# Background steps of the recurrent stage emitted at the same priority as the matrix products

## The chip, the cores and the metric

The kernel runs on one core of a Trainium2 chip. The metric is the device time of one execution in microseconds (us), the median of three runs. The engines are named as the profile names them: PE (TensorE matmul), PEld (TensorE weight load, which overlaps PE), DVE (VectorE), ACT (ScalarE), POOL (GpSimd) and SP (SyncE, which here only issues DMAs).

## The reference, cut to what matters

The whole network has two layers of mixer, cross attention and convolutional feed-forward, and then one `hybrid_layer` on 256 positions of width 1024. The change lies in that last layer:

```python
def hybrid_layer(x, ...):
    xn = rmsnorm(x, norm_mix)
    (u_rnn, u_gate, q, k_c, v_c, k_s, v_s, k_w, v_w, g_nsa, g_a, g_b) = split(xn @ w_in)
    h_a = rg_lru(causal_depthwise_conv(u_rnn, conv_w, conv_b), gate_a_w, gate_a_b, gate_x_w, gate_x_b, lru_lambda)
    y_a = h_a * gelu(u_gate)                       # recurrent branch
    y_b = nsa_mixer(q, k_c, v_c, k_s, v_s, k_w, v_w, g_nsa, ...)   # sparse attention, 16 heads
    merged = sigmoid(g_a) * (y_a @ proj_a) + sigmoid(g_b) * (y_b @ proj_b)
    h = x + merged @ w_out
    z = rmsnorm(h, norm_mlp) @ w_mlp_in
    return h + square(relu(z)) @ w_mlp_out

def rg_lru(x, w_a, b_a, w_x, b_x, lam):            # 4 blocks of 336 channels
    r, i = sigmoid(block_diag(x, w_a, b_a)), sigmoid(block_diag(x, w_x, b_x))
    log_a = -8 * r * softplus(-lam)
    u = sqrt(-expm1(2 * log_a)) * (i * x)          # first position: factor 1
    h_t = exp(log_a_t) * h_{t-1} + u_t             # scan over 256 positions
```

In `nsa_mixer` the keys and values are also compressed: `compress_blocks` runs overlapping blocks of 32 positions through a small network (`gelu(flat @ w1) @ w2`), and `rmsnorm` scales the compressed keys. Each head's scores against compressed, selected and window keys go through one softmax each, and the three results are added under gates.

## The kernel before, in words

**Products.** Each matrix product is in fp32r, split into a high and a low half on both sides, so each k step takes three matmuls (L410 to L412, `fmh`/`fml` times `wh`/`wl`). The weights are streamed by the class `Stream`. SP loads a tile (`raw`, four buffers), ACT casts it to `wh` (L220), DVE subtracts to get `wl` (L221), with four buffers of each half. `w.take(key)` hands out the next tile, and keeps the cast and the subtraction two tiles ahead of the product.

**The recurrent stage.** `block2` runs `lru_steps` over four blocks of 336 channels. A block takes 3 `ur` products (the convolution follows: one ACT activation L1295 and three DVE operations L1298 for each), 3 `ug` products (the GELU: ACT L1313 and L1315, DVE L1314 and L1316), and then the two gates, `lga` and `lgx`, each three products of 9 matmuls that ACT empties by L1328. When a block's gates are there, `lru_tail` is put on the list of background steps: exponentials (L1340), DVE L1341, tanh (L1345), a square (L1347), DVE L1348, a square root (L1350, which brings an ACT_TABLE_LOAD), DVE L1351 and L1352, the scans (L1355), L1357, and the split into `yah` (ACT L396) and `yal` (DVE L397).

**The other background steps.** `phi_steps` compresses keys and values: 8 chunks of weights in the main loop, and then as a background step the GELU on ACT (L1222, with a table load), transposes to PE and two DVE copies of one shape (L1228, L1232), the small products (L1236 for the keys, L1244 for the values), a reciprocal root by three DVE operations (L384 to L386) and 12 POOL operations (L388 to L391), the DVE scaling L1254, the transpose L1258, and the split into `ks`, whose low half is DVE L397. `nsa_units`, driven by `attend`, gives the attention: `scores` of a head pair and 128 queries, then four ticks later `probs_t` (ACT copies L1435, L1445 `pct`), two ticks later `sums` (L1454, whose result is split into a low half and `fmh`, ACT L396). In `scores`, PE computes L695 and L696, DVE adds the bias and takes the maximum (L1398 to L1411), ACT takes six exponentials (L1417), DVE scales (L1419 to L1423).

**What follows.** `ga` products (emptied by ACT L1599 into `macc`), `pa`, `gb`, `pb`, the output product and the MLP.

**Order.** PE runs in the order of the program text. The order on ACT, DVE, POOL and SP is set by a scheduler at build time, which issues ready instructions by priority; inside `high_priority(offset=n)` an instruction ranks as if written n steps earlier. Each `take` calls `tick`. It runs the `later` steps that are due (`probs_t` and `sums` among them) at an offset of `DUE` = 10, and one step of each generator in `self.back` (the tail of `phi_steps`, `lru_tail`, `attend` with `scores`) at an offset of `BACK` = 20.

Of the kernel before, what the change touches and what calls it, by code (L numbers as in the profile page):

```python
# [42 lines left out]
BACK = 20  # L43
# [130 lines left out]
class Stream:  # L174
# [3 lines left out]
    def __init__(self, tc, pool, dram, order, tick, ahead=2, raw=4, parts=4):  # L178
        self.tc, self.nc, self.pool, self.dram, self.order = tc, tc.nc, pool, dram, order
        self.after, self.until, self.tick = (), 0, tick  # L180
        self.place = {}
        self.ahead, self.raw, self.parts = ahead, raw, parts
        self.whole = ("pkv",)
        self.n = self.loaded = self.split = 0
        self.raws, self.hl = {}, {}
# [70 lines left out]
class Program:  # L256
    def __init__(self, ctx, tc, a, out):
        self.ctx, self.tc, self.nc, self.a, self.out = ctx, tc, tc.nc, a, out
        nc = self.nc
        self.base = ctx.enter_context(tc.tile_pool(name="base", bufs=1))  # L260
        self.ps = ctx.enter_context(tc.tile_pool(name="ps", bufs=1, space=bass.MemoryType.PSUM))
        wpool = ctx.enter_context(tc.tile_pool(name="w", bufs=1))
        order = []

        def add(key, lo=0, hi=None):
            n = a[key].shape[0]
            order.extend((key, c) for c in range(lo, n if hi is None else hi))

        for l in range(L1):
            if l == 0:  # L270

                add("kv0", 0, 1)
                add("qa0", 0, 1)
            for key in ("kv", "qa", "v", "u", "qb"):
                add(f"{key}{l}", 1 if l == 0 and key in ("kv", "qa") else 0)
            for b in (2, 0, 1):
                for n in range(4 * b, 4 * b + 4):
                    add(f"gate{l}", 2 * n, 2 * n + 2)
                    add(f"br{l}", n, n + 1)
            add(f"mix{l}")  # L280
            add(f"wq{l}")
            add(f"wk{l}", 2 * l, 4)
            add(f"wv{l}")
            add(f"wo{l}")
            if l == 0:
                add("wk1", 0, 1)
            add(f"upb{l}")
            add(f"up{l}")
            if l == 0:
                add(f"down{l}")  # L290
                add("wk1", 1, 2)
            else:
                for c in range(NFF):
                    for q in range(len(EARLY)):
                        if EARLY[q] == c:
                            add("q2", q, q + 1)
                    add(f"down{l}", c, c + 1)
        self.order2(add)
        self.now, self.due, self.back, self.prev = 0, [], [], None
        self.w = Stream(tc, wpool, a, order, self.tick)  # L300
        self.ident = self.base.tile([128, 128], F32, name="ident")
        make_identity(nc, self.ident)

        warm = self.sc((128, 128))
        for _ in range(WARM):
            nc.tensor.matmul(warm, self.ident, self.ident, start=True, stop=True)
# [42 lines left out]
    def tick(self):  # L349

        self.now += 1
        due = [d for d in self.due if d[0] <= self.now]
        self.due = [d for d in self.due if d[0] > self.now]
        with self.tc.high_priority(offset=DUE):
            for _, fn in due:
                fn()
        for g in list(self.back):
            with self.tc.high_priority(offset=BACK):
                if next(g, self) is self:
                    self.back.remove(g)  # L360

# [1113 lines left out]
    def block2(self, x, xs, outs):  # L1475
        nc, tc, w, a = self.nc, self.tc, self.w, self.a
        with ExitStack() as st:
# [98 lines left out]
            yb = self.fm()  # L1576
            phi = self.phi_steps(zts, w2, [k[:, :, 256:271] for k in ks], vcz, kcg)
            self.phi_done = False
            self.tbp = st.enter_context(tc.tile_pool(name="tbp", bufs=1))
            self.back.append(self.attend(self.nsa_units(qt, ks, v, vcz, gt, pcs, yb), *NSA))  # L1580
            with tc.tile_pool(name="lru", bufs=1) as lp:
# [100 lines left out]
```

## Time and profile before

| | before |
|---|---|
| runs | 1436.12 us median (1435.93 to 1438.66) |
| profiled execution | 1439.39 us, span 1437.6 us |
| PE busy | 1415.7 us (98% of the span), 9919 matmuls |
| PEld busy | 1289.7 us (90%) |
| DVE busy | 1083.4 us (75%) |
| ACT busy | 891.7 us (62%) |
| POOL busy | 47.0 us (3%) |
| PE's clock | 9 tenths or more in each of 40 slices; 1.00 from 980 to 1200 us |

PE's share says that the time is a sum of matmuls and of the few waits between them. The other engines' shares are means over the span. The recurrent stage, where the change acts, runs from about 980 to 1115 us, and the profile is read there.

### The profile page before, as it was taken

What the parts mean: (1) busy time and instruction counts of PE and PEld (TensorE: products, weight loads), DVE (VectorE), ACT (ScalarE), POOL (GpSimd) and SP (SyncE); (2) the same over time, 40 slices, a digit from 0 to 9 for tenths busy, and PEclk for the clock granted to TensorE, in tenths of its full rate; (3) what the DMA queues carried; (4) which work ended last, traced back from release to release, by engine and by line L of the source; (5) the groups of instructions that cost most, each with busy time, mean ns of one, the idle gap of its engine ahead of it and who ended that gap; (6) DMA issues with size and microseconds to landing.
All of it is one profiled execution on the core that took longest, in us unless ns stands there. A gap on an engine that the chain in (4) does not pass through costs nothing.

```text
span 1437.6 us, 26028 instructions
## 1 busy us (share of the span) xinstructions
PE 1415.7 (98%) x9919; PEld 1289.7 (90%) x9919; DVE 1083.4 (75%) x2196; ACT 891.7 (62%) x1609; POOL 47.0 (3%) x143
## 2 busy tenths in 40 slices
PE   8999999999999999999999999999999999999998
PEld 6899988899988899998889998788989999899987
DVE  6997676788857898668679986786789785866543
ACT  5876556666645486655667665464898775555432
POOL 1110000000000020000000000120100000000000
PEclk9999999999999999999999999999999999999999
DMA  8454564555556544455636557356544445645563
GB/s 316 166 191 148 191 220 136 187 187 192 182 193 218 180 152 152 137 204 175 220 132 213 196 198 260 110 171 190 167 131 142 133 145 176 208 154 197 191 206 103
DMA packets 75335, 257.63 MB, mean 179 GB/s; under 512 B 9803, under 2 KB 11211, under 8 KB 75083
## 3 DMA queue, kind: packets, MB, share of 16 engines
q1 hardware_dynamic: 75211, 255.97, 54.3%
q8 instruction: 78, 1.28, 0.3%
q14 instruction: 46, 0.38, 0.1%
HBM read 254.89 MB, written 1.05 MB: 178 GB/s over the span
## 4 chain that ended last, share of the span: by engine, by line
PE 83%; DVE 6%; ACT 5%; DMA 3%; issue 1%; POOL 1%; SPq 0%; DVEq 0%; ACTq 0%; POOLq 0%
PE mm L410 16%; PE mm L411 15%; PE mm L412 15%; PE mm L426 8%; PE mm L424 8%; PE mm L425 8%; DVE wl L221 2%; PE mm L467 2%; PE mm L469 2%; PE mm L470 2%; ACT wh L220 1%; PE tp L772 1%; PE tp L733 1%; DMA raw<-in_kv_dram 1%; PE sc L695 1%
## 5 line engine op out<-in xcount | busy, mean ns | idle before, releaser
L220 ACT CAST wh<-raw 128x1024 fp32r<-128x1024 f32 (+3 forms) x432 | 446.5, 1038 | 373.0 <-PE mm L411 124.4
L221 DVE TENSOR_TENSOR wl<-raw,wh 128x1024 fp32r<-128x1024 f32 (+3 forms) x432 | 518.0, 1204 | 210.8 <-ACT wh L220 202.3
L410 PE MATMUL mm<-fmh,wh 128*128 128x256 f32 (+1 forms) x1736 | 487.0, 281 | 2.8 <-ACT macc L1599 1.5
L412 PE MATMUL mm<-fmh,wl 128*128 128x256 f32 (+1 forms) x1736 | 483.5, 278 | 0.0
L411 PE MATMUL mm<-fml,wh 128*128 128x256 f32 (+1 forms) x1736 | 483.4, 278 | 0.0
L410 PEld LDWEIGHTS mm<-fmh,wh 128*128 128x128 f32 (+1 forms) x1736 | 324.9, 187 | 8.1 <-issue 2.9
L412 PEld LDWEIGHTS mm<-fmh,wl 128*128 128x128 f32 (+1 forms) x1736 | 324.5, 187 | 0.0
L411 PEld LDWEIGHTS mm<-fml,wh 128*128 128x128 f32 (+1 forms) x1736 | 323.7, 186 | 0.2
L424 PE MATMUL mm<-wh,fmh 128*128 128x512 f32 x200 | 79.7, 398 | 2.0 <-ACT wh L220 1.3
L425 PE MATMUL mm<-wl,fmh 128*128 128x512 f32 x200 | 78.6, 393 | 0.8 <-DVE wl L221 0.8
L426 PE MATMUL mm<-wh,fml 128*128 128x512 f32 x200 | 78.8, 394 | 0.0
L425 PE MATMUL mm<-wl,ah 128*128 128x512 f32 x164 | 63.8, 389 | 0.0
L426 PE MATMUL mm<-wh,al 128*128 128x512 f32 x164 | 63.8, 389 | 0.0
L424 PE MATMUL mm<-wh,ah 128*128 128x512 f32 x164 | 63.8, 389 | 0.0
L410 PE MATMUL mm<-oh,wh 128*128 128x256 f32 x192 | 54.1, 282 | 0.0
L412 PE MATMUL mm<-oh,wl 128*128 128x256 f32 x192 | 53.5, 279 | 0.0
L411 PE MATMUL mm<-ol,wh 128*128 128x256 f32 x192 | 53.5, 279 | 0.0
L425 PE MATMUL mm<-wl,zh 128*128 128x512 f32 x128 | 49.8, 389 | 0.0
L424 PE MATMUL mm<-wh,zh 128*128 128x512 f32 x128 | 49.8, 389 | 0.0
L426 PE MATMUL mm<-wh,zl 128*128 128x512 f32 x128 | 49.8, 389 | 0.0
L1086 ACT ACTIVATE k<-mm,featp 128x256 f32<-128x256 f32 x88 | 48.5, 558 | 0.0
L424 PEld LDWEIGHTS mm<-wh,fmh 128*128 128x128 f32 x200 | 37.6, 188 | 10.1 <-ACT wh L220 1.8
(406 smaller groups left out, 2638.3 us busy)
## 6 DMA issues: line engine op xcount, KB each, us to landing
raw<-in_up_dram SPq DMA_DIRECT2D x80, 512.0 KB, 4.3
raw<-in_gate_dram SPq DMA_DIRECT2D x48, 512.0 KB, 3.5
raw<-in_down_dram SPq DMA_DIRECT2D x44, 512.0 KB, 4.3
raw<-in_mout_dram SPq DMA_DIRECT2D x32, 512.0 KB, 4.3
raw<-in_min_dram SPq DMA_DIRECT2D x28, 512.0 KB, 4.3
raw<-in_br_dram SPq DMA_DIRECT2D x24, 512.0 KB, 3.6
raw<-in_mix_dram SPq DMA_DIRECT2D x16, 512.0 KB, 3.7
raw<-in_wo_dram SPq DMA_DIRECT2D x16, 512.0 KB, 3.5
```

Of the source, the lines that this page charges most:

```text
L220: self.nc.scalar.copy(h[:p, :w], r[:p, :w])
L221: self.last = self.nc.vector.tensor_sub(l[:p, :w], r[:p, :w], h[:p, :w].bitcast(F32))
L410: self.nc.tensor.matmul(ps, wh[:kw, c], xh[k], start=start and k == 0, stop=False)
L411: self.nc.tensor.matmul(ps, wh[:kw, c], xl[k], start=False, stop=False)
L412: self.nc.tensor.matmul(ps, wl[:kw, c], xh[k], start=False, stop=stop and k == n - 1)
L424: self.nc.tensor.matmul(outs[t], xh[:, k, r], wh[:, c], start=k == 0, stop=False)
L425: self.nc.tensor.matmul(outs[t], xh[:, k, r], wl[:, c], start=False, stop=False)
L426: self.nc.tensor.matmul(outs[t], xl[:, k, r], wh[:, c], start=False, stop=k == k_all - 1)
L467: self.nc.tensor.matmul(outs[t], xl[:, k, r], wh, start=False, stop=k == 7)
L469: self.nc.tensor.matmul(outs[t], xh[:, k, r], wh, start=k == 0, stop=False)
L470: self.nc.tensor.matmul(outs[t], xh[:, k, r], wl, start=False, stop=False)
L1086: nc.scalar.activation(y[:, i], ps, AF.Identity, bias=cb[:, c:c + 1], scale=k[1])
```

## The change

`tick` takes the offset for background steps from `self.lift`, which starts as `BACK` and is set to 0 in `block2` just before the attention is put on the list and `lru_steps` begins. With 0 no priority is opened at all. So from there on the tail of `phi_steps`, `lru_tail` and `attend` with `scores` rank where they are written. The `later` steps keep their offset of 10.

```diff
--- before.py
+++ after.py
@@ -297,6 +297,7 @@
                     add(f"down{l}", c, c + 1)
         self.order2(add)
         self.now, self.due, self.back, self.prev = 0, [], [], None
+        self.lift = BACK
         self.w = Stream(tc, wpool, a, order, self.tick)
         self.ident = self.base.tile([128, 128], F32, name="ident")
         make_identity(nc, self.ident)
@@ -355,7 +356,7 @@
             for _, fn in due:
                 fn()
         for g in list(self.back):
-            with self.tc.high_priority(offset=BACK):
+            with self.tc.high_priority(offset=self.lift) if self.lift else ExitStack():
                 if next(g, self) is self:
                     self.back.remove(g)
 
@@ -1576,6 +1577,8 @@
             yb = self.fm()
             phi = self.phi_steps(zts, w2, [k[:, :, 256:271] for k in ks], vcz, kcg)
             self.phi_done = False
+
+            self.lift = 0
             self.tbp = st.enter_context(tc.tile_pool(name="tbp", bufs=1))
             self.back.append(self.attend(self.nsa_units(qt, ks, v, vcz, gt, pcs, yb), *NSA))
             with tc.tile_pool(name="lru", bufs=1) as lp:
```

One line comes in at L300 and three by L1580, so L1328 of before is L1329 after, and L1599 is L1602; lines up to L300 keep their number. The instructions are the same, and on PE and on POOL their order is too. On ACT, the tail of `phi_steps` (the lines 1222 before, 1223 after), the tail of block 0 (L1345, L1347, L1350), the products' own casts (L220) and the activation of the `ur` products (L1295) stand so before:

```order
L1328 ACTIVATE lgx<-mm,rp_10835 112x256
L1222 ACT_TABLE_LOAD
L1222 ACTIVATE k_11771<-sc 60x256
L1345 ACTIVATE lga<-lga,cl 112x256
L1222 ACTIVATE k_11771<-sc 60x256
L1347 ACTIVATE xc<-al 112x768
L1295 ACTIVATE xc<-mm,rp_10835 112x256
L220 CAST wh<-raw 128x896
L1350 ACT_TABLE_LOAD
L1350 ACTIVATE lga<-lga 112x768
L1295 ACTIVATE xc<-mm,rp_10835 112x256
L220 CAST wh<-raw 128x896 x2
```

and so after the change:

```order
L1329 ACTIVATE lgx<-mm,rp_10835 112x256
L1346 ACTIVATE lga<-lga,cl 112x256
L1223 ACT_TABLE_LOAD
L1223 ACTIVATE k_11771<-sc 60x256
L220 CAST wh<-raw 128x896
L1296 ACTIVATE xc<-mm,rp_10835 112x256
L1348 ACTIVATE xc<-al 112x768
L1223 ACTIVATE k_11771<-sc 60x256
L220 CAST wh<-raw 128x896 x2
L1296 ACTIVATE xc<-mm,rp_10835 112x256
L1351 ACT_TABLE_LOAD
L1351 ACTIVATE lga<-lga 112x768
```

Two casts of weights and one `xc` activation have moved ahead of the second table load, that of the square root.

On DVE, at the same place, the copies out of the transposes (`k_11816` and `k_11818`) and block 0's L1351 and L1352 stand so before:

```order
L1228 COPY k_11816<-tp 128x120
L1298 SCALAR_TENSOR_TENSOR xc<-mm,rp_10835,xc 112x253
L1351 MEMSET lga 112x3
L1232 COPY k_11818<-tp 128x8x15
L1352 SCALAR_TENSOR_TENSOR lgx<-lgx,lga 112x768
L1232 COPY k_11818<-tp 128x8x15
L1298 SCALAR_TENSOR_TENSOR xc<-mm,rp_10835,xc 112x255
L221 TENSOR_TENSOR wl<-raw,wh 128x896
```

and so after:

```order
L1229 COPY k_11816<-tp 128x120
L1299 SCALAR_TENSOR_TENSOR xc<-mm,rp_10835,xc 112x254
L1233 COPY k_11818<-tp 128x8x15
L1299 SCALAR_TENSOR_TENSOR xc<-mm,rp_10835,xc 112x253
L1352 MEMSET lga 112x3
L1233 COPY k_11818<-tp 128x8x15
L1353 SCALAR_TENSOR_TENSOR lgx<-lgx,lga 112x768
L1299 SCALAR_TENSOR_TENSOR xc<-mm,rp_10835,xc 112x255
L221 TENSOR_TENSOR wl<-raw,wh 128x896
```

The second copy of `k_11818` now stands behind the memset of `lga`, and the long operation on `lgx` has moved behind that copy.

Some 15 rows on, DVE scales the compressed keys (`k_11941`) and computes the low half of `ks`, before:

```order
L1254 SCALAR_TENSOR_TENSOR k_11941<-tp,rs_y_11872,kcg 60x64 x2
L397 TENSOR_TENSOR yal<-lga,yah 112x768
L1316 SCALAR_TENSOR_TENSOR ug<-k_11924,mm 112x256
L1314 SCALAR_TENSOR_TENSOR k_11968<-k_11968,mm 112x256
L221 TENSOR_TENSOR wl<-raw,wh 112x1008
L1316 SCALAR_TENSOR_TENSOR ug<-k_11968,mm 112x256
L397 TENSOR_TENSOR ks_10848<-tp,ks_10847 128x4x15
```

and after:

```order
L1255 SCALAR_TENSOR_TENSOR k_11941<-tp,rs_y_11872,kcg 60x64 x2
L221 TENSOR_TENSOR wl<-raw,wh 112x1008
L398 TENSOR_TENSOR yal<-lga,yah 112x768
L1315 SCALAR_TENSOR_TENSOR k_11968<-k_11968,mm 112x256
L1315 SCALAR_TENSOR_TENSOR k_12004<-k_12004,mm 112x256
L221 TENSOR_TENSOR wl<-raw,wh 128x896
L1317 SCALAR_TENSOR_TENSOR ug<-k_11968,mm 112x256
L1317 SCALAR_TENSOR_TENSOR ug<-k_12004,mm 112x256
L398 TENSOR_TENSOR ks_10848<-tp,ks_10847 128x4x15
```

One weight subtraction of 128x896 and one step of the GELU (`k_12004`) have moved in between the scaling and `ks`, and the 112x1008 subtraction has come ahead of `yal`.

On ACT at the end of the recurrent stage, the copies of `probs_t`, block 3's `yah` and the first `ga` activations (`macc`) stand so before:

```order
L220 CAST wh<-raw 128x1024
L1347 ACTIVATE xc<-al 112x768
L220 CAST wh<-raw 128x1024 x2
L1350 ACT_TABLE_LOAD
L1350 ACTIVATE lga<-lga 112x768
L1435 COPY k_12561<-tp 128x4x128
L1435 COPY k_12562<-tp 128x4x128
L1445 COPY pct<-mm 128x128
L220 CAST wh<-raw 128x1024 x2
L396 CAST yah<-lga 112x768
L220 CAST wh<-raw 128x1024
L1599 ACT_TABLE_LOAD
```

and so after:

```order
L220 CAST wh<-raw 128x1024 x2
L1348 ACTIVATE xc<-al 112x768
L220 CAST wh<-raw 128x1024 x2
L1436 COPY k_12561<-tp 128x4x128
L1351 ACT_TABLE_LOAD
L1351 ACTIVATE lga<-lga 112x768
L1436 COPY k_12562<-tp 128x4x128
L1446 COPY pct<-mm 128x128
L220 CAST wh<-raw 128x1024 x2
L397 CAST yah<-lga 112x768
L397 CAST fmh<-tp 128x256
L1602 ACT_TABLE_LOAD
```

After the change four casts, not three, stand between the gates' last activations and `pct`, and the cast of `fmh` (from `sums`) has moved from behind the first `macc` activations to ahead of their table load.

On SP one load of the attention's bias (`tb`) moves behind one more load of `ga` weights.

## Rows read from the trace of the kernel before

**Rows 1.** Stretches of the span, us: busy time (instructions) of each engine, clock, DMA.
```profile
1018.00:1066.00 48.00, 43.36 (x361) 42.18 (x360) 45.79 (x114) 41.88 (x88) 4.57 (x12) 1.00 0.41 131
...
1115.00:1200.00 85.00, 85.00 (x733) 80.70 (x733) 65.52 (x302) 62.70 (x215) 0.00 (x0) 1.00 0.48 149
```

**Rows 2.** What PE waited for, 1010 to 1120 us: total, times, longest.
```profile
PE mm L410 <- ACT lga L1328: 1.6, 1, 1.6
PE mm L410 <- ACT macc L1599: 1.5, 1, 1.5
PE tp L1258 <- DVE k L1254: 1.1, 1, 1.1
PE mm L410 <- DVE nm L1411: 0.9, 1, 0.9
PE mm L412 <- DVE wl L221: 0.7, 1, 0.7
...
PE mm L410 <- ACT pct L1445: 0.3, 1, 0.3
```

**Rows 3.** ACT in time, 1018 to 1022 us: start, us, line, tiles.
```profile
1017.96 1.28 ACT L1350 ACT_TABLE_LOAD   x1
1019.26 0.85 ACT L1350 ACTIVATE lga<-lga 112x768 f32<-112x768 f32 x1
1020.01 0.55 ACT L1295 ACTIVATE xc<-mm,rp 112x256 f32<-112x256 f32 x1
1020.46 1.76 ACT L220 CAST wh<-raw 128x896 fp32r<-128x896 f32 x2
```

**Rows 4.** The second and third `ug` load of block 1: issue, DMA landing.
```profile
L193 SPq DMA_DIRECT2D raw<-in_ug_dram x2: 327/355/383, 1011.9 to 1012.3; - x2
...
DMA to landing us min/median/max: 5.7/6.4/7.2
```

**Rows 5.** PE's weight loads (PEld) in time, 1021 to 1037 us.
```profile
1021.60 1.86 PEld L1244 LDWEIGHTS tp<-w,k 128*128 128x128 f32 x16 [0.56 <-PE tp L1236]
...
1036.62 0.19 PEld L696 LDWEIGHTS sc<-ks,qt 128*128 128x128 f32 x1
```

**Rows 6.** DVE in time, 1021 to 1036 us.
```profile
1021.20 0.28 DVE L1232 COPY k<-tp 128x120 f32<-128x120 f32 x1
1021.40 0.47 DVE L1298 SCALAR_TENSOR_TENSOR xc<-mm,rp,xc 112x255 f32<-112x255 f32 x1
1021.79 1.08 DVE L221 TENSOR_TENSOR wl<-raw,wh 128x896 fp32r<-128x896 f32 x1
...
1026.83 0.14 DVE L386 TENSOR_SCALAR rs_y<-rs_t 60x1 int32<-60x1 int32 x1
...
1027.28 0.41 DVE L1248 COPY vcz<-tp 64x256 f32<-64x256 f32 x1
...
1032.55 0.47 DVE L1254 SCALAR_TENSOR_TENSOR k<-tp,rs_y,kcg 60x64 f32<-60x64 f32 x2 [0.62 <-POOL rs_y L391]
1032.94 0.94 DVE L397 TENSOR_TENSOR yal<-lga,yah 112x768 fp32r<-112x768 f32 x1
...
1035.92 0.20 DVE L397 TENSOR_TENSOR ks<-tp,ks 128x60 fp32r<-128x60 f32 x1
```

**Rows 7.** POOL in time, 1027 to 1032.5 us (12 rows in all).
```profile
1027.04 0.19 POOL L388 TENSOR_TENSOR rs_t<-rs_y 60x1 f32<-60x1 f32 x1 [57.74 <-DVE rs_y L386]
1027.31 0.18 POOL L389 TENSOR_TENSOR rs_t<-rs_t,rs_v 60x1 f32<-60x1 f32 x1
...
1030.76 1.21 POOL L389 TENSOR_TENSOR rs_t<-rs_t,rs_v 60x1 f32<-60x1 f32 x1
```

**Rows 8.** ACT in time, 1107 to 1117 us.
```profile
1107.52 2.02 ACT L220 CAST wh<-raw 128x1024 fp32r<-128x1024 f32 x2
...
1112.42 1.28 ACT L1599 ACT_TABLE_LOAD   x1
...
1116.91 0.37 ACT L396 CAST fmh<-tp 128x256 fp32r<-128x256 f32 x1
```

## The prediction

> **What bounds the kernel now.** I read the page first (its shares are in the table above): PE is busy nearly all of the span, so the time is PE's work plus its few waits. The windows come next, over the stretch in which the change reorders anything: from 1018 to 1066 us PE is busy 43.36 of 48 us, from 1115 to 1200 it is busy all 85 [rows 1]. In the first of these DVE is busy 45.79 and ACT 41.88 of 48 us, so all three are nearly full, and whatever is put ahead of something on ACT or DVE is paid for by what stands behind it. The view of PE's waits says what PE stood for [rows 2]. Four of its six rows are products waiting for their own helpers: 1.6 us for ACT's `lga` eviction, 0.9 for DVE's maxima to free a PSUM buffer, 0.7 for `wl`, 1.5 for `macc`, in all 4.7 us. The other two are waits for background steps: 1.1 for the scaled keys (L1254), 0.3 for `pct`. So both kinds of wait exist, 6.1 us in all. Less priority for background can shorten the first kind and must lengthen the second. The timelines of ACT, DVE, POOL and PEld at three places then show who stands behind whom.
>
> **The change part by part.** Instructions and PE's order are the same, so only PE's waits can change. I follow the three places where PE needs a background result, and then the places where it needs a product's result.
>
> *A, the end of the compression, before L1244.* PE's L1244 starts at 1021.60 [rows 5], right after the second copy L1232 of DVE at 1021.20 [rows 6]. After the change that copy stands behind the memset, which waits for ACT's square root. Before, ACT began the table load for it at 1017.96 and the root at 1019.26, which took 0.85 [rows 3]. Now two casts (1.76 together) and one `xc` activation (0.45, from 1020.01 to the next start at 1020.46) stand ahead of that load [rows 3], less 0.1 of overlap between starts: load at 17.96 + 1.67 + 0.45 = 20.1, if the weights are there. They are not: the two loads were issued at 1011.9 and 1012.3 and landed after 5.7 and 7.2 us [rows 4], at 17.6 and 19.5. The second cast can begin at 19.5, ends at 20.4, the activation at 20.85. The load then begins 2.9 us later than before, the root ends at 20.1 + 2.9 = 23.0, the copy (0.28) follows, and PE goes on at 23.45. That is **+1.85 us**. If the weights' landing does not bind, it is +1.0; these are A's bounds.
>
> *B, the scaled keys, before L1258.* DVE ended the reciprocal root's three operations at 1026.83, 5.63 us behind the second copy [rows 6]. Between the two now come also L1353 and `xcl` (both the size of `yal`, 0.94) and two copies L1249 (0.41 each), while one L1299 (0.47) and one L221 (1.08) leave [rows 6]. By durations that is +1.15; starts follow each other about 0.1 sooner than durations say (the L1298 row begins at 21.40, the next at 21.79), so +1.0. With the copy at 23.15, L387 is at 23.15 + 5.63 + 1.0 = 29.8. POOL's 12 operations follow. Undisturbed, starts lie 0.27 apart, 3.2 us in all; before, the chain ran from 1027.04 to DVE's L1254 at 1032.55, 5.5 us [rows 6, 7], since three of the operations were stretched; one of them took 1.21 us while DVE ran an L221 over the same time [rows 7]. Beside the chain there now stand two such DVE operations (L221 and L1358) and not three, as `xcl` has gone ahead; I take 5.0 us. Bounds are 3.5, nothing stretched, and 5.7, nothing won. L1255 starts at 34.8, and PE's transpose follows as it did before (32.55 to 33.13, less its 1.1 of waiting on PE's own clock, puts PE's own arrival at 32.0 + 1.85 = 33.9): 35.4 instead of 33.1. PE is now 2.25 late, **+0.4** to A; the chain's bounds make that −1.1 (its wait here gone) to +1.1. [...]
>
> *C, `ks`, before the first scores.* Before, the low half of `ks` was written at 1035.92 and 0.20 long, and PE read it at 1036.62 [rows 5, 6]: 0.5 us to spare. Now one L221 of 128x896 (1.0) and one GELU step (0.4) come in between L1255 and `ks`: 1.4 later against PE, which is 0.5 beyond the slack. **+0.9**, a new wait on L695 or L696; bounds 0.5 and 1.3, a GELU step either way.
>
> *D, from 1058 to 1066.* The wait of 0.7 for `wl` should go, since that L221 comes ahead of the scores' maxima. The 1.6 and the 0.9 stay, because the six exponentials still stand ahead of the `lga` eviction on ACT, and `yah`, which waits for DVE's L1358, now comes ahead of the exponentials; I price it like `yal`, 0.94 [rows 6]. PE's lateness does not shrink here either. DVE had 2.2 us idle in these 48 [rows 1], and between L387 and L1255 it now has 2.8 us of work (L1315, L221, L1358, L1317) to fill POOL's 5.0, so 2.2 idle in place of the 0.6 in that row [rows 6]: nothing is left to catch up with. 0.94 − 0.7 is **+0.2**, with −0.7 (`yah` fits into a gap) and +0.9 (the 0.7 stays) as bounds.
>
> *E, the end of the stage.* One more cast (2.02 for two [rows 8]) stands ahead of `pct`, so its wait goes from 0.3 to 1.2, +0.9. And `fmh`, the result of the attention's sums, now stands ahead of the table load for `macc` (at 1112.42, 1.28) [rows 8]; it waits for PE's sums and takes 0.37, so the 1.5 becomes 1.9, +0.4. **+1.3** in all, bounds 0 and 1.6.
>
> Behind 1115 PE has no idle time in the window and the same work; the reordered steps there lie beside its matmuls, with DVE at 65.5 and ACT at 62.7 of 85 us [rows 1], so 20 us of cover before they cost anything. The bias load that one `ga` load passes on SP is wanted by DVE only at the next group's scores; I cost it at nothing, and if that cover were gone, it would cost at most one load's 5.7 to 7.2 us [rows 4].
>
> The sum is 1.85 + 0.4 + 0.9 + 0.2 + 1.3 = **+4.7 us**. The profiled execution took 1439.39, so it would take 1444.1. That execution lay 3.27 above the median of 1436.12, so on the median I predict **1440.8 us**, 0.33% slower. The bounds of A to E give −0.3 (all low) to +6.8 (all high); since they will not all fall on one side, I take half of each way, +2.2 to +5.7, or 1438.3 to 1441.8.
>
> **The rivals.**
>
> *The delay is eaten (no change).* PE enters 1058 about 3.1 us late. It waits 3.2 us there (1.6 + 0.9 + 0.7) [rows 2], and a PE that comes late would not wait, if ACT and DVE have kept their own time. Then only D's and E's +1.5 remain: 1437.6, within 0.2% (2.9 us, about what a measurement of this kernel can tell from no change). For it: the waits are big enough. Against it: ACT's and DVE's steps there hang on products that PE computes late, and DVE has no reserve. It decides itself at the `lga` eviction: if PE's wait of 1.6 shrinks by as much as PE is late, this rival holds.
>
> *The products' waits vanish (faster).* Casts, subtractions and evictions now rank ahead of the recurrence and the attention, so the 4.7 us of waits of products for their own helpers [rows 2] could go, with A to C hidden: 1436.1 − 4.7 = 1431.4. [...] For it: the `lga` eviction stands behind the attention's exponentials on ACT, and the maxima are background work on DVE. Against it: in the new order the exponentials still come ahead of `lga`, and `fmh` ahead of `macc`; only the 0.7 for `wl` goes. It decides itself by whether the exponentials come behind the eviction in time: with that 1.6 and the 0.7 gone, and A to C not above 1 us together, the sign turns unless E costs its full 1.3.
>
> *PE's new waits run deeper (much slower).* If C's wait also delays the scores' maxima, and these the exponentials, D grows by the same 0.9 again and E by one more cast (1.0) that it queues behind: 4.7 + 0.9 + 1.0 = +6.6, 1442.7. This belongs to the slower cases.
>
> **How the numbers follow.** The forecast has 0.52, the deeper waits 0.14, the eaten delay 0.22, the vanishing waits 0.12. "Slower" begins at 1436.12 + 2.87 = 1439.0, "faster" ends at 1433.25; of the forecast's 0.52 some 0.04 fall below 1439.0, so slower has 0.62, the same 0.26, faster 0.12. The likeliest gives 1440.8, with a range of its own of 1438.3 to 1441.8. The range for 8 in 10 goes down over the eaten delay to 1434.5, which leaves out most of the faster case, and up to 1443.6, with the deeper waits' 1442.7 in it.
>
> **What would show it.** In the changed profile: PE stands about 1.9 us longer before L1245 than it did before L1244; the wait at L1259 stays at 1 to 1.5; a new wait for `ks` of about 0.9 at L695 or L696; `pct` about 1.2; `macc` about 1.9; no wait for `wl` near 1060. PE's waits from 1010 to 1120 are then some 11 us, not 6.1. I am wrong if L1245 follows the first copy without a wait, if the 1.6 for `lga` is gone, or if new waits show behind 1120.

## The result, and the profile after

The changed kernel takes 1446.13 us (median of 6 runs, 1444.52 to 1452.38) against 1436.8 us before (6 runs, 1435.87 to 1440.05). The ratio is 1.0063, with an interval of 1.0041 to 1.0084: slower, as forecast, but by 9 us and not by 4.7, and outside the range. In a second measurement the same kernel gave 1.0040 (1.0021 to 1.0059), with medians of 1445.73 and 1439.66, 6.1 us apart. The profiled execution took 1445.37 us with a span of 1443.6, 6.0 more than the one before.

The windows of the changed kernel's profile, by stretch (busy time of PE, PEld, DVE, ACT, POOL, then the granted clock, DMA share and GB/s), answer to [rows 1]:

```profile
1018.00:1063.00 45.00, 41.70 (x349) 40.87 (x350) 39.45 (x102) 36.83 (x69) 3.66 (x12) 1.00 0.40 125
1063.00:1068.00 5.00, 1.27 (x10) 1.05 (x9) 5.00 (x13) 4.86 (x18) 0.00 (x0) 0.97 0.32 98
1068.00:1071.00 3.00, 3.00 (x16) 3.00 (x15) 2.33 (x7) 3.00 (x6) 0.00 (x0) 0.50 0.43 142
1071.00:1106.00 35.00, 34.86 (x296) 33.64 (x295) 27.95 (x81) 31.06 (x73) 0.00 (x0) 1.00 0.46 147
1106.00:1125.00 19.00, 16.04 (x137) 14.89 (x136) 16.48 (x44) 15.60 (x32) 0.00 (x0) 1.00 0.41 129
1125.00:1200.00 75.00, 75.00 (x648) 70.70 (x647) 59.20 (x283) 56.91 (x194) 0.00 (x0) 1.00 0.45 140
```

PE stands still for most of 1063 to 1068, and then, from 1068 to 1071, it is busy all the time and yet issues 16 matmuls in 3 us, where the stretch behind it issues 25 in the same time: the clock is at 0.50, the lowest that any window of these profiles shows. The kernel before has 1.00 in the windows of [rows 1]. PE's waits after the change, to be read against [rows 2] (total, times, longest, in us):

```profile
PE mm L411 <- DVE ug L1317: 3.7, 1, 3.7
PE mm L411 <- ACT macc L1602: 2.2, 1, 2.2
...
PE tp L1259 <- DVE k L1255: 1.4, 1, 1.4
PE tp L1245 <- DVE k L1233: 1.3, 1, 1.3
PE mm L411 <- ACT pct L1446: 0.8, 1, 0.8
...
PE sc L697 <- DVE ks L398: 0.4, 1, 0.4
PE tp L1227 <- ACT k L1223: 0.4, 1, 0.4
```

The view of before has one row more than [rows 2] shows, a wait of 0.4 at the very place of step A, so its waits are 6.5 us in all and not 6.1; after the change they are 10.2.

```profile
PE tp L1244 <- DVE k L1232: 0.4, 1, 0.4
```

The waits for `lga` (1.6), for the maxima (0.9) and for `wl` (0.7) are gone, and in their place stands one of 3.7. It ends with DVE's L1317, which empties a PSUM buffer of the GELU. PE in time, changed kernel:

```profile
1063.22 0.28 PE L412 MATMUL mm<-xcl,wh 112*112 112x256 f32 x1
1063.34 0.28 PE L413 MATMUL mm<-xch,wl 112*112 112x256 f32 x1
1067.35 0.37 PE L411 MATMUL mm<-xch,wh 112*112 112x256 f32 x1 [3.73 <-DVE ug L1317]
```

ACT in the same stretch of the changed kernel, the time and its length first:

```profile
1063.14 0.83 ACT L397 CAST yah<-lga 112x768 fp32r<-112x768 f32 x1 [0.49 <-DVE lga L1358]
1063.88 0.51 ACT L1418 ACTIVATE k<-k,nm 128x256 f32<-128x256 f32 x1
...
1066.44 0.71 ACT L1316 ACTIVATE k<-k 112x256 f32<-112x256 f32 x2
1067.05 0.82 ACT L1329 ACTIVATE lga<-mm,rp 112x256 f32<-112x256 f32 x2
```

And ACT in the kernel before, at the same place of the program:

```profile
1055.50 0.83 ACT L396 CAST yah<-lga 112x768 fp32r<-112x768 f32 x1 [1.97 <-DVE lga L1357]
...
1061.04 0.51 ACT L1417 ACTIVATE k<-k,nm 128x256 f32<-128x256 f32 x1
```

After the change `yah` comes right ahead of the six exponentials and itself waits for DVE's L1358. The exponentials run from 1063.88 to 1066.44; two tanh of the GELU stand behind them, L1317 on DVE behind those, and PE behind L1317.

Since PE's order is the same in both, the n-th matmul of one trace can be set against the n-th of the other. The difference of their starts, zero at 985 us, is how late PE is. The table gives it in us; its columns are times of the kernel before (1024 is behind L1244, 1034 behind L1258, 1044 behind the first scores, 1073 behind the stretch D, 1125 the end of the stage):

| kernel | 1024 | 1034 | 1044 | 1058 | 1073 | 1106 | 1125 | 1420 |
|---|---|---|---|---|---|---|---|---|
| before, second profile | -0.3 | -0.3 | -0.3 | -0.3 | -0.3 | -0.3 | -0.3 | -0.3 |
| changed | 1.4 | 1.8 | 2.7 | 2.6 | 4.2 | 4.7 | 6.0 | 6.0 |
| changed, second profile | 2.1 | 2.4 | 3.3 | 3.2 | 5.5 | 6.0 | 7.3 | 7.3 |
| phi0 | 0.2 | 2.8 | 4.3 | 4.3 | 4.6 | 5.2 | 5.4 | 5.4 |
| tail0 | -0.5 | 1.3 | 2.7 | 2.6 | 3.5 | 3.5 | 3.5 | 3.5 |
| att0 | 0.5 | 0.5 | 0.5 | 0.4 | -0.9 | 1.3 | 3.8 | 3.8 |
| yah1 | 5.1 | 6.1 | 6.6 | 6.5 | 5.5 | 6.0 | 8.8 | 8.8 |
| lift10 | 0.5 | 1.1 | 2.7 | 2.6 | 4.6 | 4.5 | 6.7 | 6.7 |
| fill | 1.1 | 1.5 | 2.3 | 2.2 | 2.4 | 2.8 | 5.4 | 5.4 |
| fill4 | 1.4 | 1.8 | 2.6 | 2.5 | 4.2 | 4.6 | 8.4 | 8.4 |
| fill28 | 3.4 | 4.5 | 5.0 | 4.9 | 5.3 | 5.7 | 8.2 | 8.2 |
| flat345 | 0.3 | 0.3 | 0.3 | 0.2 | 2.6 | 2.6 | 2.6 | 2.6 |
| soft2 | 0.2 | 0.2 | 0.2 | 0.2 | -0.7 | 0.4 | 0.5 | 0.5 |

Behind 1125 nothing is added in any of them. The changed kernel's two profiles give +6.0 and +7.3 us, or ratios of 1.0042 and 1.0051, inside the interval of each measurement.

### The profile page after: what moved, and what is told of

It reads as the page before. It is cut to its first block, busy times and chain, and to the rows that moved or that the text cites. A ratio compares the mean times of both kernels' runs of the same rounds, so it can differ in the third digit from the quotient of the medians.

```text
span 1443.6 us, 26049 instructions
## 1 busy us (share of the span) xinstructions
PE 1419.0 (98%) x9919; PEld 1292.8 (90%) x9919; DVE 1083.3 (75%) x2196; ACT 892.0 (62%) x1609; POOL 46.6 (3%) x143
## 4 chain that ended last, share of the span: by engine, by line
PE 80%; DVE 9%; ACT 5%; DMA 3%; issue 2%; POOL 1%; SPq 0%; DVEq 0%; ACTq 0%; POOLq 0%
PE mm L411 15%; PE mm L412 15%; PE mm L413 15%; PE mm L425 7%; PE mm L426 7%; PE mm L427 7%; DVE wl L221 3%; PE mm L468 2%; PE mm L470 2%; PE mm L471 2%; ACT wh L220 1%; PE tp L773 1%; PE tp L734 1%; DMA raw<-in_kv_dram 1%; PE tp L565 1%
## 5 line engine op out<-in xcount | busy, mean ns | idle before, releaser
L220 ACT CAST wh<-raw 128x1024 fp32r<-128x1024 f32 (+3 forms) x432 | 446.7, 1038 | 377.4 <-PE mm L412 123.2
L221 DVE TENSOR_TENSOR wl<-raw,wh 128x1024 fp32r<-128x1024 f32 (+3 forms) x432 | 518.4, 1205 | 214.9 <-ACT wh L220 204.4
L426 PEld LDWEIGHTS mm<-wl,fmh 128*128 128x128 f32 x200 | 37.6, 188 | 9.1 <-DVE wl L221 1.3
```

The lines of the kernel that those rows point to most:

```text
L220: self.nc.scalar.copy(h[:p, :w], r[:p, :w])
L221: self.last = self.nc.vector.tensor_sub(l[:p, :w], r[:p, :w], h[:p, :w].bitcast(F32))
L426: self.nc.tensor.matmul(outs[t], xh[:, k, r], wl[:, c], start=False, stop=False)
```

## The experiments

**The changed kernel again, and its parts.** `after_again` has no edit.

> The changed kernel once more, with a second profile. If the profiled execution told all of it (waits +4.5 us, clock +1.5 us), the ratio comes out near 1.0042 and the profile again shows the 3.7 us wait and a granted clock of 0.5 for about 3 us behind it. If more of the loss lies in clock falls that vary from execution to execution, the ratio stays near 1.0063 and this profile shows a different, longer stretch at the low clock.

The ratio was 1.0040 (1.0021 to 1.0059). The long waits are the same to 0.1 us, except that the 1.4 at L1259 is gone and 0.3 at L1237 has come in. The clock fell in two places of the stage, here in the windows of this second profile (columns as above):

```profile
1024.00:1030.00 6.00, 6.00 (x41) 6.00 (x40) 5.97 (x13) 1.67 (x2) 0.00 (x0) 0.72 0.26 79
1030.00:1066.00 36.00, 34.02 (x284) 33.20 (x282) 30.84 (x83) 31.69 (x66) 3.86 (x12) 1.00 0.39 116
1066.00:1073.00 7.00, 4.75 (x22) 4.75 (x23) 6.02 (x15) 6.97 (x21) 0.00 (x0) 0.53 0.55 163
```

So the ratio took the first branch of the expectation and the profile the second. Of the 1.3 us that this execution lost more, half is ahead of 1034, where a cast waited 0.4 for late weights, and half in D, where the clock stayed low for longer. The fall at 1025 itself took PE's lateness from 1.8 to 3.4 us and was for the most part paid back: PE came later to L1259, did not wait there, and stood at 2.4 behind it.

Three kernels give up the priority for one kind of background step alone. In `tick`, with one name in the tuple (`'phi_steps'` for phi0, `'lru_tail'` for tail0, `'attend'` for att0; the edit moves the lines behind it on by one more, so that L1260 here is L1258 of before):

```diff
-            with self.tc.high_priority(offset=self.lift) if self.lift else ExitStack():
+            lift = self.lift if g.gi_code.co_name in ('phi_steps',) else BACK
+            with self.tc.high_priority(offset=lift) if lift else ExitStack():
```

> Only the end of the compression loses its priority; recurrences and attention keep theirs. Order theory: steps A to C alone, +1.5 to +2.5 us, no wait over 2 us near 1064 and a clock of 1.00. Lateness theory (the long wait is the lateness of A to C handed on): +6 us or more, with a wait over 3 us near 1064.

> Only the recurrences lose their priority. Order theory: the root behind the casts delays L1245 by about 0.9 us, the end of the recurrence of block 1 comes behind the attention's maxima on DVE and holds the exponentials on ACT, so the wait near 1064 is over 2.5 us; the end of the stage is as before. +3 to +5 us in all, with a clock fall if the wait passes 3 us. Lateness theory: PE is only 1 us late there, so the wait near 1064 is no longer than 2 us and the sum +1 us.

> Only the attention loses its priority. Order theory: A to C stay as before; near 1064 the first lga eviction and a tanh of the GELU now come ahead of the exponentials, so the waits there fall from 3.2 to about 1; the end of the stage loses 1.2 as in the changed kernel: -1 us in all, from -2.5 to +0.5. Lateness theory: the same, as PE is not late. If the attention's late maxima make the long wait, it shows here: over 3 us near 1064 and +3 us or more.

phi0 gave 1.0030 (1.0015 to 1.0046), tail0 1.0010 (0.9997 to 1.0024), att0 1.0009 (0.9994 to 1.0024). In phi0 PE reached 1058 4.3 us late, later than in the changed kernel, and no wait over 2 us followed near 1064. So the long wait is not lateness handed on, and that theory falls. The order theory was wrong on the size of phi0 and on its clock. L1260 waited 3.6 us, where POOL's chain was stretched further, and behind that wait the clock fell, which took PE from 2.8 us late at 1034 to 4.3 at 1044. A window of phi0, and its POOL rows:

```profile
1042.00:1044.00 2.00, 2.00 (x11) 2.00 (x10) 0.98 (x3) 1.43 (x4) 0.00 (x0) 0.50 0.79 244
```

```profile
1032.25 1.70 POOL L390 TENSOR_TENSOR rs_t<-rs_y 60x1 f32<-60x1 f32 x1 [59.43 <-DVE rs_y L388]
1034.03 0.18 POOL L391 TENSOR_TENSOR rs_t<-rs_t,rs_v 60x1 f32<-60x1 f32 x1
1034.30 1.20 POOL L392 TENSOR_SCALAR rs_t<-rs_t 60x1 f32<-60x1 f32 x1
1035.58 0.78 POOL L393 TENSOR_TENSOR rs_y<-rs_y,rs_t 60x1 f32<-60x1 f32 x1
```

In phi0 four long DVE operations (L1359, `xcl`, an L221, `yal`) run beside the chain, which takes 6.3 us from its first row at 1032.25 to DVE's L1256 at 1038.53. In the kernel before there were three and 5.5 us [rows 6, 7], in the changed kernel two and 4.6. tail0 waits 2.8 us at L1260 and loses 0.9 in D, with one wait of 2.4 us for the GELU and a low clock behind it, from 1062 to 1066: less than the 2.5 us that were expected, and less than the 3 us that its expectation wanted for a fall. Its profile lies at +3.5, its ratio lower. att0 wins 1.3 us in D, as expected, and loses it and more behind: 2.2 by 1106, and 2.4 at the end of the stage, where the clock is low from 1119 to 1123. The three parts come to 12.7 us in their profiles, against 6.0 for the whole: they do not add up.

**The control.** `before_again` is the kernel before.

> The kernel before, unchanged, as a control. Ratio 1.000; the interval says what these measurements can tell apart. If the falls of the clock belong to the changed order, this profile shows none behind the first 20 us. If they come by chance to any kernel, it shows some here too.

1.0007 (0.9992 to 1.0022), the same waits as [rows 2] within 0.2 us, and no low clock up to the end of PE's work.

That holds for this execution, whose mean granted clock is 0.999 of full speed, and not for the kernel: 3 of the 12 runs here and 22 of the 92 others of the kernel before, taken beside the experiments, had 0.997 or less, which is over 7 us at 0.50 (an estimate: 0.0025 of 1437 us, times two). So falls do come by chance to the kernel before too; what the change does is bring more of them. The mean over all runs is 0.9983 to 0.9984 in the three groups of the kernel before and 0.9955 and 0.9951 in the two measurements of the changed kernel. By that, the changed kernel spends some 9 us more at 0.50 in each execution (an estimate: 0.0031 of 1440 us, times two, as the low windows show 0.50). The first profile of the changed kernel, with 0.999, has the fewest falls of its six runs, whose others lie between 0.993 and 0.996.

Single runs of this one kernel lay between 1433.9 and 1446.5 us, so a ratio here tells some 2 us at best, and the profiles' stage times tell more.

**Is it the standing still that lowers the clock?** Extra matmuls ahead of the third `lga` product of block 2, 28 of them in fill and fill28, 4 in fill4:

```diff
                 for n in range(3):
+                    if b == 2 and key == "lga" and n == 2:
+                        fill = self.tp((128, S))
+                        for _ in range(28):
+                            nc.tensor.matmul(fill[:RW], wt[0][:RW, :RW], xh[:, 0], start=True, stop=True)
                     ps = self.mm((128, S))
```

> The changed kernel with 28 extra matmuls of 112x256, whose result nobody reads, on PE just ahead of the lga product that waits 3.7 us. They take about 3.3 us (0.117 each, as the products beside them). If the fall of the clock comes from PE standing still, the wait shrinks to under 0.6 us, the granted clock stays at 1.00 from 1066 to 1073, and the products behind start 1.5 to 2 us earlier against those ahead than in the changed kernel. If the clock falls for another reason, the low clock is seen there all the same and nothing is gained.

> The changed kernel with 4 extra matmuls ahead of the lga product that waits, in place of 28. The order on ACT, DVE and SP is row for row that of the kernel with 28. If standing still is what lowers the clock, PE here waits some 3 us, the granted clock falls to 0.5 behind it, and the stage is 1.5 to 2 us longer than with 28 extra matmuls. If the clock follows something else, the two profiles show the same clock and the stage is at most 0.5 us different.

> The kernel with 28 extra matmuls again, beside the one with 4. Theory: clock 1.00 from 1063 to 1075, stage 1.5 to 2 us shorter than with 4, ratio about 0.001 lower, which is no more than these intervals can show. Rival: no difference in clock or stage.

fill gave 1.0042 (1.0024 to 1.0060), and in the later measurement fill28 1.0045 (1.0027 to 1.0063) and fill4 1.0071 (1.0055 to 1.0086). Windows of fill4:

```profile
1068.00:1071.00 3.00, 0.98 (x6) 0.98 (x7) 3.00 (x11) 3.00 (x12) 0.00 (x0) 0.90 0.69 174
1071.00:1074.00 3.00, 3.00 (x17) 3.00 (x17) 2.35 (x6) 1.89 (x5) 0.00 (x0) 0.53 0.44 146
1074.00:1077.00 3.00, 3.00 (x29) 3.00 (x28) 0.57 (x2) 2.88 (x7) 0.00 (x0) 1.00 0.83 235
```

And of fill28:

```profile
1068.00:1071.00 3.00, 2.28 (x20) 2.06 (x19) 3.00 (x12) 3.00 (x10) 0.00 (x0) 1.00 0.71 240
1071.00:1074.00 3.00, 3.00 (x29) 3.00 (x28) 1.76 (x2) 3.00 (x7) 0.00 (x0) 1.00 0.47 137
1074.00:1077.00 3.00, 3.00 (x28) 3.00 (x27) 1.68 (x2) 3.00 (x7) 0.00 (x0) 1.00 0.60 207
```

The waits that end with L1317, first in fill4, then in fill28:

```profile
PE mm L411 <- DVE ug L1317: 3.5, 2, 3.3
PE mm L411 <- DVE ug L1317: 0.9, 2, 0.7
```

These two kernels have the same rows in the same order on ACT, DVE and SP. With 4 extra matmuls PE stands still for 3.3 us and the clock falls; with 28 it does not stand still for longer than 0.7 us and the clock stays. From 1058 to 1073 fill4 loses 1.6 us (2.5 to 4.2), fill 0.1 and fill28 0.4. That is the price of the low clock at this place: 1.3 to 1.5 us. All runs bear the clock out: its mean is 0.9984 over the 12 runs of fill and 0.9971 over the 9 of fill28, against 0.9958 over the 6 of fill4. fill's whole ratio shows no gain over the changed kernel, because its order on ACT and DVE differs from the changed kernel's from 1069 on: `macc` waits 3.0 us, in fill4 and fill28 too, and in all three the clock falls there.

**One step, and nothing else.** flat345 is the kernel before, with the priority taken from the scores of the attention's second unit alone (tick 345):

```diff
+FLAT = (345,)
...
-            with self.tc.high_priority(offset=BACK):
+            low = g.gi_code.co_name == "attend" and self.now in FLAT
+            with ExitStack() if low else self.tc.high_priority(offset=BACK):
```

> The kernel before, with one single step without priority: the scores of the attention's second unit (5 ACT and 25 DVE rows move, all near 1060). Weight subtractions come ahead of its maxima, the exponentials stay ahead of the lga eviction. Theory: the waits for wl (0.7) and for the maxima (0.9) go, and the one for lga grows by what PE comes earlier, so the three together stay at 2.5 to 3.5 us, the clock at 1.00, ratio 0.999 to 1.001. If lost priority is bad at this place by itself, as in the changed kernel, they grow to over 3.5 us in one wait and the clock falls.

1.0012 (1.0001 to 1.0023). Its wait near 1060, a window behind it, and rows of PE:

```profile
PE mm L412 <- ACT lga L1330: 3.1, 1, 3.1
```

```profile
1064.00:1066.00 2.00, 2.00 (x11) 2.00 (x11) 2.00 (x7) 1.00 (x3) 0.00 (x0) 0.50 0.84 231
```

```profile
1060.19 0.27 PE L414 MATMUL mm<-xch,wl 112*112 112x256 f32 x1
1063.59 0.55 PE L412 MATMUL mm<-xch,wh 112*112 112x256 f32 x1 [3.13 <-ACT lga L1330]
...
1064.16 0.41 PE L414 MATMUL mm<-xch,wl 112*112 112x256 f32 x1
1064.37 0.41 PE L412 MATMUL mm<-xch,wh 112*112 112x256 f32 x1
```

The three waits of before (0.9, 0.7 and 1.6, in all 3.2) have become one of 3.1. As waits that is no loss. But behind it the matmuls start 0.21 us apart (1064.16 to 1064.37) and not 0.12 as ahead of the wait in the changed kernel (1063.22 to 1063.34), and PE comes out 2.4 us later than before. The expectation had the waits right and the clock wrong: it fell without the waits growing.

The other profiles agree at this place. In D the clock fell in all six whose longest single wait there is 2.4 us or more (tail0, lift10, flat345, fill4 and the two of the changed kernel), and stayed in all eight where it is 1.6 or less, among them phi0 and the kernel before with 3.2 us of waits in three pieces. But it is one profile of flat345: over its 12 runs the mean granted clock is 0.9978, against 0.9984 for the 26 of the kernel before beside it, so the fall does not come in each of its executions.

**The late recurrence step alone.** yah1 is the changed kernel with the old priority for the last step of block 1's recurrence:

```diff
-        nc.vector.scalar_tensor_tensor(tr, tr, 0.5, ug, op0=OP.mult, op1=OP.mult)
...
-        self.split(h, l, tr)
+        with self.tc.high_priority(offset=BACK) if b == 1 else ExitStack():
+            nc.vector.scalar_tensor_tensor(tr, tr, 0.5, ug, op0=OP.mult, op1=OP.mult)
...
+            self.split(h, l, tr)
```

> The changed kernel, with only the last step of block 1's recurrence (L1358, yah, yal) given its old priority. Theory: this step, late on DVE, holds the exponentials on ACT and they the GELU and the lga evictions; with it back, the 3.7 us wait falls to under 1.5 us, the clock stays at 1.00 there, and about 3 to 4 us of the loss are gone (ratio near 1.001 to 1.002). Rival: the attention's own late maxima make the wait; then it stays over 2.5 us and the ratio near 1.005.

The wait of 3.7 is gone as expected: 1.0, 0.8 and 0.5 in its place, and PE wins 1.0 us between 1058 and 1073 where the changed kernel loses 1.6. The ratio is 1.0033 (1.0018 to 1.0048), less of a gain than expected, because `macc` waits 3.2 us at the end with a fall of the clock behind it, and because in this execution PE was 3.3 us late at L1245 and the clock was low from 1019 to 1029, which left it 6.1 late at 1034. The ACT rows and the landing of the `ug` load issued at 1008.1 tell why L1245 came late, and the window shows the clock:

```profile
1014.33 0.94 ACT L220 CAST wh<-raw 128x896 fp32r<-128x896 f32 x1 [1.12 <-DMA raw<-in_ug_dram]
1016.54 0.94 ACT L220 CAST wh<-raw 128x896 fp32r<-128x896 f32 x1 [1.27 <-DMA raw<-in_ug_dram]
```

```profile
L193 SPq DMA_DIRECT2D raw<-in_ug_dram x1: 383/383/383, 1008.1 to 1008.1; - x1
...
DMA to landing us min/median/max: 8.3/8.3/8.3
```

```profile
1022.00:1024.00 2.00, 2.00 (x11) 2.00 (x11) 2.00 (x4) 0.00 (x0) 0.00 (x0) 0.50 0.15 22
```

ACT stands still for two loads, with the activation and the square root behind them. A load that comes late now delays the compression, on which PE waits.

**Two tries at a better order.** lift10 sets `self.lift` to 10 in place of 0. soft2 is the kernel before with the exponentials of the second unit, and what follows them, put into a `later` step:

```diff
+            if self.now == 345:
+                self.later(2, soft)
+            else:
+                soft()
```

> The changed kernel with an offset of 10 in place of 0 from the recurrent stage on. By its order on ACT and DVE the compression stands as before, yah comes early, the first lga eviction comes ahead of the exponentials, pct ahead of the root, and only macc stays behind fmh. If PE's waits are all there is, it has waits of some 5 us in the stage, no fall of the clock, and a ratio of 0.998 to 1.001. If the lost priority as such costs time, it lies between the two kernels, near 1.003.

> The kernel before, with the exponentials of the attention's second unit (and what follows them) written two ticks later, at the offset of 10. One tanh of the GELU and one lga eviction come ahead of the exponentials. Theory: the 1.6 us wait for lga shrinks to under 1, the others stay, ratio 0.998 to 1.0005. If the exponentials' delay is handed on to the copies of the probabilities and the end of the stage, macc and pct wait over 1 us longer, and nothing is gained.

lift10 gave 1.0029 (1.0013 to 1.0044), a miss: `lga` waited 3.0 us in two pieces, `macc` 2.6, and the clock fell three times in the stage. soft2 gave 1.0004 (0.9986 to 1.0023): the wait for `lga` shrank from 1.6 to 0.4 as expected, but between 1073 and 1090 a new wait of 0.8 us for a weight cast came in. Neither beats the kernel before.

## Why the prediction was wrong, point by point

**A (+1.85).** Measured at the start of L1245, 1.4 and 1.8 in the two profiles of the changed kernel. (The 2.1 of the table's 1024 has some of the low clock in it.) The mechanism is the one named; DVE and ACT rows of the first of them, where the weights did not bind:

```profile
1020.41 1.28 ACT L1351 ACT_TABLE_LOAD   x1
1021.71 0.84 ACT L1351 ACTIVATE lga<-lga 112x768 f32<-112x768 f32 x1
```

```profile
1022.60 0.28 DVE L1233 COPY k<-tp 128x120 f32<-128x120 f32 x1 [0.48 <-issue]
...
1029.46 0.15 DVE L387 TENSOR_SCALAR rs_y<-rs_t 60x1 int32<-60x1 int32 x1
...
1034.29 0.47 DVE L1255 SCALAR_TENSOR_TENSOR k<-tp,rs_y,kcg 60x64 f32<-60x64 f32 x2 [1.89 <-POOL rs_y L392]
```

The table load began at 1020.41, forecast 1020.1 without and 1020.85 with the landing. A wait of 0.4 at L1227, for the second GELU half, was not foreseen; it is not added, since L1245 waits for the copy either way. But the range given for A was too narrow: with late loads, in yah1 and fill28, whose order is the changed kernel's at this place, it was 3.3 and 2.4, and a low clock, behind L1237 in yah1 and behind L1245 in fill28, made PE later still.

**B (+0.4) and C (+0.9)** held. L387 came at 1029.46 (forecast 1029.8), L1255 at 1034.29 (1034.8), and PE lost 0.3 and then 0.9 us at the two places, 0.7 of the 0.9 at L697. (C's sum is right, but 1.4 is 0.9 beyond the slack and not 0.5; and with nothing won B's chain is 5.5 by its rows and not 5.7.) That the chain on POOL gets shorter because one long DVE operation left it was right. In the kernel before, three of POOL's rows took 0.78 to 1.21 us beside three such operations; in the changed kernel two took 0.79 and 1.02, beside an L221 and L1358; the other rows took 0.18 or 0.19. The three chains of 4.6, 5.5 and 6.3 us with two, three and four such operations beside them agree.

**D (+0.2)** is the step that failed. As a sum of waits it is right: from 1058 to the matmul at 1067.35 PE lost 0.1 us more than before. It failed in the sentence that the 1.6 and the 0.9 stay and the 0.7 goes: the three became one of 3.7 us, so that the 1.6 for `lga` was gone, which the prediction itself named as a sign of being wrong. And the prediction priced a wait by its length alone, with PE's clock at nothing. After the 3.7 the clock fell, and PE lost 1.5 us more in the first profile and 2.2 in the second. flat345 shows, in one profile, that this takes no longer waits, only their joining. fill4 against fill28 shows that here it takes PE standing still: 3.3 us with a fall behind it, 0.7 us with none. The profiles agree: behind single waits of 2.4 to 3.7 us in D the lowest windows of 2 us show 0.50 to 0.56, and behind the 1.6 us of [rows 2] the clock is 1.00. What sets the clock is not shown. The clock is a term of its own beside A to E, and the sum did not have it.

**E (+1.3)** held in sum, 1.3 from 1106 to 1125 in both profiles, but not in its parts: `pct` waits 0.8 (forecast 1.2), `macc` 2.2 (1.9).

**The rivals.** That the delay is eaten is excluded: in phi0, PE came 4.3 us late to 1058 and won nothing back by 1073. That the products' waits vanish came true in D alone, and not in the changed kernel: where only the attention lost its priority (att0) PE won 1.3 us there, in yah1 1.0 and in soft2 0.9.

**The sum.** A to E as waits come to 1.4 + 0.3 + 0.9 + 0.1 + 1.3 = 4.0 and 0.5 at small places between, 4.5 us, against 4.7 forecast. That the two are so close is in part luck: A came out 0.4 short, and the 0.5 that no term had made up for it. The clock adds 1.5 in the first profile, which makes 6.0; in the second it adds 2.2 at that place, and with the late load in A and the fall at 1025 the sum is 7.3. The medians lie 9.3 us apart in one measurement and 6.1 in the other. The some 9 us more at 0.50 that the granted clocks of all runs give would cost up to half of that, some 4 us, where the first profile has 1.5; with the 4.5 of waits that is 8.5, an estimate from those figures. Where the falls lie in executions without a profile is not known, so the rest stays open.

## What to carry to other kernels

Where PE is the bound, add up its waits, but price each also by what PE's clock does behind it: in the profiles here three waits of 0.9, 0.7 and 1.6 us cost 3.2, and one of 3.1 cost 2.4 us more. Here a reordering that joined waits, or that put a step PE waits for behind work that hangs on a DMA (step A: 1.4 to 3.3 us, where the durations say 1.0), cost more than the moved instructions' durations say, and cost differently from run to run. The step to look for is the background one in the middle of a chain of three engines (here `yah` ahead of the exponentials ahead of the GELU ahead of a PSUM buffer): with its priority back (yah1) the long wait was gone, though the whole stage was not better than before in any order tried.

## What the runs showed of the hardware that was not expected

The low clock came behind single waits of 2.4 (tail0, lift10), 3.1 (flat345), 3.3 (fill4) and 3.7 us, but in the second profile of the changed kernel also at 1025, behind waits of 0.3, 0.3 and 1.4 us within some 5 us; in the first profile the same places, with 0.4 and 1.3, kept 1.00. And behind the wait of 2.2 for `macc` it fell in att0 and not in either profile of the changed kernel. So the length of one wait does not settle it. It then lasted between 3 and 10 us, the longest in yah1. And kernels whose first 980 us are the same instructions in the same order came to the same matmul there with up to 9 us of difference (against the first profile of before, 4.9 us earlier in tail0 and 3.9 later in fill): more than the change itself costs in either profile, and the reason why the stage's own times were compared.
